# Decoder trunk in fp32 on one core: group norms by a matrix of ones, the first output projection in two halves, both first mixers reordered, a state update tied behind the weight splits

## The chip, the cores and the metric

One core of a Trainium2 chip. Time is device microseconds (us) of one execution of the whole program. TensorE does matrix products, VectorE (DVE), ScalarE (ACT) and GpSimd (POOL) elementwise work; SyncE (SP) issues the loads, POOL the stores. Each engine works through its own queue in order and waits there for what an instruction needs from others.

## What is computed

One step of a four-layer decoder: 256 prompt tokens and 8 single tokens of running sequences (264 columns together), width 1024. Layers: RWKV-7, gated linear attention (GLA), short convolution, multi-scale pooling, each followed by a squared-ReLU MLP of width 4096. The parts that the change touches:

```python
# RWKV-7: 16 heads of 64; S is a head's 64 x 64 state
def step(S, inp):
    r_t, w_t, k_t, v_t, a_t, b_t = inp
    sa = jnp.einsum('bhvk,bhk->bhv', S, a_t)
    S = S * w_t[:, :, None, :] + sa[..., None] * b_t[:, :, None, :] + v_t[..., None] * k_t[:, :, None, :]
    return S, jnp.einsum('bhvk,bhk->bhv', S, r_t)
...
mean = jnp.mean(y, axis=-1, keepdims=True)            # over a head's 64 channels
var = jnp.mean(jnp.square(y - mean), axis=-1, keepdims=True)
yn = ((y - mean) * lax.rsqrt(var + RWKV_GN_EPS)).reshape(B, L, D) * ln_w + ln_b
out = ((yn + bonus) * g) @ wo
...
h = h + out
h = h + jnp.square(jax.nn.relu(rmsnorm(h, norm_ffn[i], NORM_EPS) @ w_up)) @ w_down
```

## The kernel before

Activations lie with channels on partitions: 8 tiles of 128 channels by 264 columns, a `slab` holding four of them. All tiles called slab share one pool of 32 buffers; weights pass through `wr` (tag wraw) and `wh` (tags whi, wlo), three buffers each, nine in all. TensorE's accumulators are eight banks, three tagged `acc` and five `ps`.

Most projections use a split form (`mm3`): a weight block of 512 KB is loaded (wraw), rounded to a high part (whi, `put`, L180) and its remainder (wlo, `tt`, L188), usually on ScalarE and VectorE, and three matmuls of 264 columns add up high x high, high x low and low x high. The projections k, v and r of the first mixer (`proj_full`) instead use plain fp32 matmuls, which the trace shows as two records each.

Instructions are emitted by Python generators in the order of a plan, and a scheduler then fixes the order in each engine's queue, with the order of emission as priority among what it takes to be ready. In `RWKV_PLAN` a letter names a generator and each occurrence advances it by a step: X, V, R mix the operands of the projections k, v, r; h and G belong to the gate; s solves the triangular systems; S and O are state and output steps of a chunk of 64 tokens; D, Y, n, l serve the decode tokens; N is a group norm. `RWKV_ENGINES` and `GLA_ENGINES` say by site and number which engine takes an elementwise operation (A, V or G for ACT, DVE, POOL). `GLA_PLAN` hangs such steps behind the four parts of each pair of projections; s, o, u, l there are split, output, update and load of the decode states, A the attention blocks, L and K their decay factors (gZQ and gEX).

The group norm (`gnorm(g)`, L848 on) works on three groups of columns, group 0 (tokens 0 to 127), group 1 (128 to 191 and the decode tokens) and group 2 (192 to 255): centre by a matmul (`cen`, tile pc), square, sum each head's 64 channels into 16 rows (`sel`, tile pv), take the reciprocal root on 16 partitions (`rsq`: logarithm and exponential on ACT, three closing operations on DVE, L362 to L364), spread it over 128 partitions (`spread`, tile pr), copy, multiply, apply weight, bias and gate, and split the result into the parts xh and xl that `mixer_out` (L408) feeds to `wo_proj`. Its results go with `norm_prep` into the MLP's input X; `ffn` begins with `rstd` over the squares.

`decode_update` (L930) updates the decode tokens' state in four quarters of five DVE operations each on 128 x 1024 elements (L938 to L946). It is advanced by one step per pair of the first MLP's up projection (`next(self.later)`). It loads a quarter's state (wS) when the quarter before begins, and stores each when done.

## Time and profile before

| | us |
|---|---|
| median of three runs | 1348.36 (1346.07 to 1354.53) |
| the profiled execution | 1348.23 |
| its span, first to last instruction | 1346.5 |
| TensorE busy | 1290.8 |
| VectorE busy | 908.5 |
| ScalarE busy | 573.0 |
| GpSimd busy | 399.5 |

In the rows, PE is TensorE's matmuls and PEld its weight loads, DVE VectorE, ACT ScalarE, POOL GpSimd; L with a number is a line of the program above, and where a helper records the operation (put, tt) many operations share a line and are told apart by their tiles. Tile names stand as out<-in. "x16" counts instructions. A matmul is pipelined: its length in a row is longer than the distance to the next one. PEclk is the clock granted to TensorE as a share of full speed. Behind `<-` stands what ended a wait.

### The profile page before, as it was taken

To read this page: it belongs to the slowest core of one execution; us is meant where nothing else is said; L and a number is where in the kernel's file an instruction comes from. 1 tells how busy PE (TensorE), PEld (TensorE's weight loads), DVE (VectorE), ACT (ScalarE), POOL (GpSimd) and SP (SyncE) were. 2 spreads that over 40 slices of the span, in tenths; PEclk is the share of its full clock that TensorE was granted. 3 is DMA by queue.
4 is the path that set the end of the run, shared out by engine and by line. 5 is a ranking of instruction groups with operands and counts; after the bars stand their busy time and mean duration, and the time that the engine had idled before them with its cause. 6 is when DMAs were issued, how large, how long until landed. Compare 5 with 4: busy or idle time off the path is not lost.

```text
span 1346.5 us, 25575 instructions
## 1 busy us (share of the span) xinstructions
PE 1290.8 (96%) x10332; PEld 1237.0 (92%) x10332; DVE 908.5 (67%) x1392; ACT 573.0 (43%) x931; POOL 399.5 (30%) x420
## 2 busy tenths in 40 slices
...
GB/s 275 95 115 74 48 49 9 111 176 194 190 215 204 174 142 109 141 172 117 175 181 186 184 177 183 175 178 170 179 186 178 183 256 128 126 181 180 188 176 92
DMA packets 161880, 211.10 MB, mean 157 GB/s; under 512 B 11569, under 2 KB 116945, under 8 KB 161762
## 3 DMA queue, kind: packets, MB, share of 16 engines
...
## 4 chain that ended last, share of the span: by engine, by line
PE 80%; DVE 7%; DMA 5%; issue 3%; POOL 2%; SPq 1%; ACT 1%; DVEq 0%; ACTq 0%; POOLq 0%
PE dacc L234 11%; PE dacc L232 11%; PE dacc L233 11%; PE acc L232 10%; PE acc L234 10%; PE acc L233 10%; PE acc L272 5%; DMA wS<-in_state_wkv 2%; DVE wlo L188 1%; DMA wraw<-in_ffn_up 1%; DMA g1a<-in_rwkv_g 1%; PE pr L866 1%; PE pss L373 1%; PE pAr L802 1%; PE pQ L761 1%
## 5 line engine op out<-in xcount | busy, mean ns | idle before, releaser
L188 DVE TENSOR_TENSOR wlo<-wraw,whi 128x1024 fp32r<-128x1024 f32 x318 | 400.7, 1263 | 225.6 <-ACT whi L180 224.3
L180 ACT CAST whi<-wraw 128x1024 fp32r<-128x1024 f32 x319 | 333.6, 1049 | 407.9 <-PE dacc L233 183.1
L234 PE MATMUL acc<-xh,wlo 128*128 128x264 f32 x1408 | 398.8, 287 | 8.5 <-DVE wlo L188 8.4
L232 PE MATMUL acc<-xh,whi 128*128 128x264 f32 x1408 | 397.1, 286 | 2.9 <-DVE ggs L1145 2.7
L233 PE MATMUL acc<-xl,whi 128*128 128x264 f32 x1408 | 399.4, 286 | 0.0
L233 PE MATMUL dacc<-sl,whi 128*128 128x264 f32 x1024 | 288.9, 284 | 0.0
L232 PE MATMUL dacc<-sh,whi 128*128 128x264 f32 x1024 | 288.0, 284 | 0.0
L234 PE MATMUL dacc<-sh,wlo 128*128 128x264 f32 x1024 | 284.2, 284 | 1.4 <-DVE wlo L188 1.4
L234 PEld LDWEIGHTS acc<-xh,wlo 128*128 128x128 f32 x1408 | 264.7, 189 | 11.3 <-DVE wlo L188 10.0
L232 PEld LDWEIGHTS acc<-xh,whi 128*128 128x128 f32 x1408 | 264.0, 189 | 6.2 <-DVE ggs L1145 3.1
L233 PEld LDWEIGHTS acc<-xl,whi 128*128 128x128 f32 x1408 | 265.4, 189 | 0.6
L403 POOL TENSOR_TENSOR fs<-ft 128x264 f32<-128x264 f32 x128 | 135.6, 1063 | 262.6 <-DVE ft L399 257.5
L233 PEld LDWEIGHTS dacc<-sl,whi 128*128 128x128 f32 x1024 | 192.7, 188 | 0.0
L232 PEld LDWEIGHTS dacc<-sh,whi 128*128 128x128 f32 x1024 | 192.5, 188 | 0.0
L234 PEld LDWEIGHTS dacc<-sh,wlo 128*128 128x128 f32 x1024 | 190.0, 188 | 1.6 <-DVE wlo L188 1.6
L346 POOL TENSOR_TENSOR sq<-sq 128x264 f32<-128x264 f32 x40 | 36.8, 920 | 382.8 <-ACT sq L342 382.0
L272 PE MATMUL acc<-xm,wfull 128*128 128x264 f32 x384 | 89.1, 388 | 0.0
L272 PEld LDWEIGHTS acc<-xm,wfull 128*128 128x128 f32 x384 | 72.0, 190 | 13.7 <-issue 1.9
L399 DVE SCALAR_TENSOR_TENSOR ft<-acc,rstd 128x264 f32<-128x264 f32 x128 | 54.0, 427 | 37.5 <-PE acc L234 37.2
L404 DVE TENSOR_TENSOR sl<-fs,sh 128x264 fp32r<-128x264 f32 x128 | 58.0, 470 | 26.7 <-POOL fs L403 26.7
L401 ACT ACTIVATE sh<-ft 128x264 fp32r<-128x264 f32 x128 | 51.1, 420 | 47.2 <-DVE ft L399 44.9
L233 PE MATMUL dacc<-xl,whi 128*128 128x264 f32 x192 | 53.8, 289 | 1.0 <-POOL xl L188 0.7
...
## 6 DMA issues: line engine op xcount, KB each, us to landing
wraw<-in_ffn_up SPq DMA_DIRECT2D x128, 512.0 KB, 3.7
wraw<-in_ffn_down SPq DMA_DIRECT2D x128, 512.0 KB, 3.3
wraw<-in_gla_w_in SPq DMA_DIRECT2D x24, 512.0 KB, 3.7
wraw<-in_conv_w_in SPq DMA_DIRECT2D x24, 512.0 KB, 3.4
wfull<-in_rwkv_wk SPq DMA_DIRECT2D x8, 512.0 KB, 8.4
wfull<-in_rwkv_wv SPq DMA_DIRECT2D x8, 512.0 KB, 4.7
...
wfull<-in_rwkv_wr SPq DMA_DIRECT2D x8, 512.0 KB, 3.5
```

The costliest lines, as they stand in the source:

```text
L180: return e.copy(out, x) if scale is None else e.activation(out, x, AF.Copy, scale=scale)
L188: return self.on(site, i).tensor_tensor(out, x, y, op=op)
L232: mm(acc, h, xh, start=first, stop=False)
L233: mm(acc, h, xl, start=False, stop=False)
L234: mm(acc, l, xh, start=False, stop=last)
L272: self.nc.tensor.matmul(accs[mi][:, :NT], w[:, kk, mi * 128:(mi + 1) * 128], self.at(X, k), start=(k == 0), stop=(k == 7))
L346: self.nc.gpsimd.tensor_tensor(ss[0], ss[0], sq, op=ALU.add)
L373: nc.tensor.matmul(pp[:, :NT], self.C("ones"), x, start=f, stop=l)
L399: nc.vector.scalar_tensor_tensor(t, acc, 0.0, rs, op0=ALU.max, op1=ALU.mult)
L401: nc.scalar.activation(h, t, AF.Square)
L403: nc.gpsimd.tensor_tensor(s, t, t, op=ALU.mult)
L404: nc.vector.tensor_tensor(l, s, h.bitcast(F32), op=ALU.subtract)
```

## The change

Four things are done together. The group norm sums each head's squares with the block matrix of ones `blk`, which leaves the sum on all of its head's partitions; the reciprocal root is then taken on 128 partitions for four tiles at once, and spreading and copying fall away. The result stays fp32, unsplit. The output projection of the first mixer becomes `out_part(h)` with plain fp32 matmuls, once for columns 0 to 127 (U in the plan, eight steps among the norms of groups 2 and 1) and once for the other 136 (B, eight steps at the end); the eight weight blocks (128 columns each) are loaded in the first half and kept for the second. Each half sums its squares, makes its part of the reciprocal root `rsf` and writes its part of the MLP's input. The update of the decode state gets an order: none of its operations may be placed ahead of the low part of the last split emitted before it; two quarters are loaded at the end of the mixer, the others when a quarter has been stored. The plans and the engine strings of the first two mixers change; for the site zq, for instance, POOL's turns go from the third, fourth and eighth to the fourth and seventh, for ek from the third, fifth, seventh and eighth to the third, seventh and eighth, and xs goes from POOL, DVE to DVE, DVE.

```diff
@@ -224,7 +224,7 @@
     def wsplit(self, w, shape, place=None, site=("A", "V"), i=0):
         h, l = [place(shape, n, F32R) if place else self.wh.tile(shape, F32R, name=n, tag=n) for n in ("whi", "wlo")]
         self.put(site[0], i, h, w)
-        self.tt(site[1], i, l, w, h.bitcast(F32), ALU.subtract)
+        self.lo_ins = self.tt(site[1], i, l, w, h.bitcast(F32), ALU.subtract)
         return h, l
 
     def mm3(self, acc, h, l, xh, xl, first, last):
@@ -384,7 +384,7 @@
 
     def ffn(self, li, ss, X, next_prep, between):
         nc = self.nc
-        rs = self.rstd(ss)
+        rs = self.rstd(ss) if isinstance(ss, list) else ss
         up, down = self.I["ffn_up"][li], self.I["ffn_down"][li]
         sh = [self.slab([128, 4, NT], "sh", F32R) for _ in range(8)]
         sl = [self.slab([128, 4, NT], "sl", F32R) for _ in range(8)]
@@ -425,26 +425,26 @@
 
...
 RWKV_PLAN = """
-G R X h X X e X x0 R l0 X x1 X z z h x2 X h X z h a z z h a h a x3 x4 k0 h a k1 a a k1 k0 k1 a k1 a h z z z R t k0
-d5 d4 d2 k0 d3 R d6 d1 R k2 K0 d0 V V R k2 R V k2 R V k2 V d7 k3 V V V K0 v0 K0 v0 v0 I0 k3 k3 k3 v0 K1 v1 I0 v1 v1
-K1 I0 v1 K1 v2 v2 w00 v2 I1 v2 v3 I1 v3 v3 r0 v3 r0 I1 w01 r0 w10 y0 r0 s b1 b0 r1 r1 T100 T000 s r1 r1 w11 r2 r2 r2
-s b3 g3 r2 r3 b2 r3 s T001 r3 T101 b4 g2 s r3 b7 g4 T010 b5 g7 s l1 s D0 D1 b6 T011 g0 T110 y1 l2 g6 s S00 w21 S01
-S01 g1 S00 S01 T111 l3 O0 w30 S00 S11 w20 D2 O0 S10 D0 w31 S11 S10 S11 S21 D2 D3 D3 O1 w41 S10 w40 S21 S21 S20 S20
-S20 O2 O2 S30 D1 g5 S31 S31 O1 S30 S31 N0 S30 N0 Y P n O3 O3 N1 N1 N0 N1 N2 N2 N2 N0 N2 N1
+h X X X X X X h G R e a h X X x0 R l0 h x1 z h z h z x2 h z a z z a x3 x4 k0 a h k1 a a k1 k0 k1 a k1 a z z R t k0
+d5 d4 d2 k0 d3 V R d6 d1 R k2 K0 V d0 V R k2 R V k2 R V k2 V d7 k3 V V K0 v0 K0 v0 v0 I0 k3 k3 k3 v0 v1 K1 I0 v1 v1
+I0 K1 v1 v2 K1 v2 w00 v2 I1 v2 v3 I1 v3 w10 v3 r0 v3 I1 r0 r0 y0 r1 r1 w11 r0 s b1 b0 r1 r1 r2 T000 s r2 b2 r2 s b3
+g3 T100 r2 r3 r3 w01 s T001 r3 T101 b4 g2 s r3 b7 g4 T010 b5 g7 s l1 s D0 b6 D1 g0 T011 T110 l2 g6 s y1 S00 w21 T111
+S01 S01 w30 g1 S00 S01 S00 S11 l3 w20 S10 w31 S11 S10 D2 S11 O0 O0 S10 D0 S21 w41 D2 S21 S20 O1 w40 S21 S20 S31 S20
+S30 O1 g5 N0 D3 S30 O2 D3 N0 S31 S31 S30 N0 O3 O2 O3 D1 Y N0 N2 U n U N2 P N2 N1 U N2 N1 U U U N1 U N1 U B B B B B B
+B B
 """
 
 
@@ -834,7 +834,7 @@
         V.scalar_tensor_tensor(at(bg, m), at(bg, m), k.P("lnb", m), pg, op0=ALU.add, op1=ALU.mult)
         k.put("gT", m, at(gT, m), pg, k.P("lnw", m))
 
-    Y = k.new_x()
+    Y = two("yo")
 
 
     GROUPS = (((0, 128),), ((128, 64), (NP, NS)), ((192, 64),))
@@ -854,26 +854,20 @@
             mm(pc[a], k.C("cen"), y_tile(g, a), start=True, stop=True)
             A.activation(q[a], pc[a], AF.Square)
         yield
-        pv = k.bank("pv")[0:16, :n]
-        for m in range(8):
-            mm(pv, sel[:, m], at(q, m), start=(m == 0), stop=(m == 7))
-        r, x, c = [k.t(nm, [16, n]) for nm in ("gnr", "gnx", "gnc")]
-        k.rsq(r, pv, 1.0 / 64, k.epsg[0:16], 64e-5, c, x)
+
+        rc = [k.slab([128, 2, 4, n], "gnr") for _ in range(2)]
+        for a in range(2):
+            pv = k.bank("pv")[:, :4 * n].rearrange("p (m t) -> p m t", m=4)
+            mm(pv, k.C("blk"), q[a], start=True, stop=True)
+            k.rsq(rc[a][:, 0], pv, 1.0 / 64, k.epsg, 64e-5, rc[a][:, 1], rc[a][:, 0])
         yield
         for a in range(2):
-            pr = k.bank("pr")[:, :4 * n].rearrange("p (m t) -> p m t", m=4)
-            for mi in range(4):
-                mm(pr[:, mi], spread[:, 4 * a + mi], r, start=True, stop=True)
-            k.put("gq", g * 2 + a, q[a], pr)
-            V.tensor_tensor(q[a], pc[a], q[a], op=ALU.mult)
+            V.tensor_tensor(q[a], pc[a], rc[a][:, 0], op=ALU.mult)
             at0 = 0
             for i, (lo, w) in enumerate(GROUPS[g]):
                 xv, cs, j = q[a][:, :, at0:at0 + w], slice(lo, lo + w), g * 4 + a * 2 + i
                 k.tt("gg", j, xv, xv, gT[a][:, :, cs], ALU.mult)
-                k.tt("gb", j, xv, xv, bg[a][:, :, cs], ALU.add)
-                h, l = Y[0][a][:, :, cs], Y[1][a][:, :, cs]
-                k.put("gh", j, h, xv)
-                k.tt("gl", j, l, xv, h.bitcast(F32), ALU.subtract)
+                k.tt("gb", j, Y[a][:, :, cs], xv, bg[a][:, :, cs], ALU.add)
                 at0 += w
             yield
 
@@ -929,23 +923,28 @@
 
     def decode_update():
 
-        decode_load(0)
+
+        def op(out, x, y, o):
+            k.queue_after(V.tensor_tensor(out, x, y, op=o), k.lo_ins)
+
+        for qv in range(2):
+            decode_load(qv)
         yield
         for qv in range(4):
-            if qv < 3:
-                decode_load(qv + 1)
             S, vs, T = wS[qv], slice(qv * 16, (qv + 1) * 16), [k.slab([128, 16, 64], "wT") for _ in range(2)]
-            V.tensor_tensor(T[0], vb(vt[:, 4, vs]), kb(3), op=ALU.mult)
+            op(T[0], vb(vt[:, 4, vs]), kb(3), ALU.mult)
             yield
-            V.tensor_tensor(T[1], vb(sav[:, vs]), kb(2), op=ALU.mult)
+            op(T[1], vb(sav[:, vs]), kb(2), ALU.mult)
             yield
-            V.tensor_tensor(T[0], T[0], T[1], op=ALU.add)
+            op(T[0], T[0], T[1], ALU.add)
             yield
-            V.tensor_tensor(S, S, kb(1), op=ALU.mult)
+            op(S, S, kb(1), ALU.mult)
             yield
-            V.tensor_tensor(S, S, T[0], op=ALU.add)
+            op(S, S, T[0], ALU.add)
             for h2 in range(2):
                 k.store(Sdst[h2][:, :, qv * 1024:(qv + 1) * 1024], S[OWN[h2]].rearrange("p v k -> p (v k)"))
+            if qv < 2:
+                decode_load(qv + 2)
             yield
 
     def decode_rotate():
@@ -1038,6 +1037,36 @@
         for par in range(2):
             k.store(O["wkv_p"][OWN[par]], XV[4][par][OWN[par], :, 0, :])
 
+
+
+    wo, Xf = {}, k.new_x()
+    rsf = k.t("rsf")
+
+    def out_part(h):
+        cs, n = ((slice(0, 128), 128), (slice(128, NT), NT - 128))[h]
+        ss = []
+        for m in range(8):
+            if h == 0:
+                wo[m] = k.wfull(I["rwkv_wo"][:, m * 128:(m + 1) * 128].rearrange("(k p) c -> p k c", p=128), [128, 8, 128])
+            acc = k.bank("dacc", "ps" if m % 2 else "acc")[:, :n]
+            for kk in range(8):
+                mm(acc, wo[m][:, kk, :], at(Y, kk)[:, cs], start=(kk == 0), stop=(kk == 7))
+            x, xh, xl, g, sq = k.hT[:, m, cs], at(Xf[0], m)[:, cs], at(Xf[1], m)[:, cs], k.P("ffn0", m), k.t("sq", [128, n])
+            V.tensor_tensor(x, acc, x, op=ALU.add)
+            A.activation(sq, x, AF.Square)
+            if m in (0, 6, 7):
+                ss.append(sq)
+            else:
+                G.tensor_tensor(ss[0], ss[0], sq, op=ALU.add)
+            A.activation(xh, x, AF.Copy, scale=g)
+            V.scalar_tensor_tensor(xl, x, g, xh.bitcast(F32), op0=ALU.mult, op1=ALU.subtract)
+            if m == 7:
+                p = k.bank("pss")[:, :n]
+                for i, y in enumerate(ss):
+                    mm(p, k.C("ones"), y, start=(i == 0), stop=(i == 2))
+                k.rsq(rsf[:, cs], p, 1.0 / 1024, k.eps6, 1e-6, k.t("rsc", [128, n]), k.t("rsq", [128, n]))
+            yield
+
     def pair(n, X, pr, evac):
         if FULL[n]:
             return k.proj_full(I["rwkv_w" + n], pr * 256, X, lambda mi, acc: evac(pr * 2 + mi, acc))
@@ -1047,34 +1076,35 @@
     work = {"e": decay_low, "z": decay_logs, "a": rates, "X": lambda: operand(2, "k", Xk), "h": gate_in, "t": table, "d": decays, "K": keys, "I": inner,
             "V": lambda: operand(3, "v", Xv), "R": lambda: operand(0, "r", Xr), "s": solve, "b": after_r, "T": transposed, "G": gate_load,
             "g": gate, "w": values, "x": new_xv, "y": decode_rows, "l": decode_load, "D": decode, "Y": decode_out, "n": decode_rotate, "N": gnorm, "S": state_step,
-            "O": output_step, "P": state_out, "k": lambda i: pair("k", Xk, i, ev_k),
+            "O": output_step, "P": state_out, "U": lambda: out_part(0), "B": lambda: out_part(1), "k": lambda i: pair("k", Xk, i, ev_k),
             "v": lambda i: pair("v", Xv, i, ev_v), "r": lambda i: pair("r", Xr, i, ev_r)}
     k.issue(work, RWKV_PLAN)
     k.later = decode_update()
-    return k.mixer_out(I["rwkv_wo"], 0, Y)
+    next(k.later)
+    return rsf, Xf
 
 
 GLA_ENGINES = {
-    "gwh": "VAAAVVVAAAAVVVAAVAAAAVVV", "gwl": "VVVGGVVGGVVGGVVGGVGVVGGG", "lsh": "VV", "lsl": "VG", "zq":
-    "VVGGVVVG", "ek": "VVGVGVGG", "att": "VAAAAA", "xs": "GV", "ax": "A", "kt": "AV", "vt": "AAVVAVAA", "ot":
-    "VVVA", "sp": "AA", "sh": "AVAVAVAAAAAAAAGV", "sl": "VVVGGVVGGVVGVGGV", "km": "AGVVGVAVGAVVGVGV", "nq": "GGVG",
-    "go": "GVVGVGGG", "gy": "VVGGVVGG", "yh": "VVVVAAVA", "yl": "GGGGVGGG",
+    "gwh": "VAAAVVVAAAAVVVAAVAAVAVVV", "gwl": "VVVGGVVGGVVGGVVGGVGGVGGV", "lsh": "VA", "lsl": "VG", "zq":
+    "VVVGVVGV", "ek": "VVGVVVGG", "att": "VAAAAA", "xs": "VV", "ax": "A", "kt": "AV", "vt": "AAVVAAAA", "ot":
+    "AVVA", "sp": "VA", "sh": "AGAVAVAAVAAAAAAV", "sl": "VVVGGVVGGVVGVGGV", "km": "AGVVGVAAGAVVVVVV", "nq": "GGGV",
+    "go": "VGVGVGGG", "gy": "VVVGGVGG", "yh": "VVVVAAVA", "yl": "VGGGVGGG",
 }
 
 GLA_PLAN = [
     ("q0", "", "", "", "G"),
     ("q1", "", "Z0", "", ""),
-    ("k0", "", "", "l0", "Z1 L00 L01 K01"),
-    ("k1", "", "", "Z2", "L10"),
-    ("v0", "", "", "", "L02 L11 K11 D"),
+    ("k0", "", "", "l0", "Z1 L00 L01 K01 Z2"),
+    ("k1", "", "", "L10", ""),
+    ("v0", "", "", "", "D L02 L11 K11"),
     ("v1", "", "k", "L03", "K00"),
-    ("v2", "K02", "L12", "A17 K03 A02 l1 l2 K12 A03 A01 s01 K10 A00", ""),
-    ("v3", "", "V1 A06 l3 A04 A05 L13", "s11 s00 s21 o00 W0 F K13", "A10 s10 o01 s20 W1 u00 o11 o10 s31 l4"),
-    ("g0", "o21 X", "u10 u11 A13 s30 u01 A16 s41 A12 l5 s40 s51 l6 o20 s50 u30 o31 s60 o30 l7 o40 o41", "u20 A15 u21 u31 s61 s71", "u40 V0 A14 u50 V3 u51 o50 u41 A11"),
-    ("g1", "s70 A07 u60 V2 Y u70 o60 T1 O1 O0 o70", "", "N0 T0 N1 O2 o51 o61 o71 u61 u71 a0 a1 M0 M1", ""),
-    ("g2", "N2 O3 N3", "b M2 c M3 g3", "", "g0 g1"),
-    ("g3", "g2 g5", "", "g4 S0", ""),
-    ("wo", "g7 g6 S1"),
+    ("v2", "K02", "L12 K10 l1", "A17 K03 A02 l2 K12 A03 A01 s01", "A06 A00 V1"),
+    ("v3", "", "l3 A04 A05 L13", "s00 o00 W0 l4 F K13 s11", "s10 s31 o01 o11 s20 W1 s21 u00 o10"),
+    ("g0", "o21 A10 X", "u10 u11 A13 s30 u01 A16 s41 A15 l5 s40 s51 l6 o20 s50 u30 o31 s60 o30 l7 o40 o41", "u20 A12 u50 u21 u31 s61 s71", "u40 A14 V0 u41 A11 o50 A07"),
+    ("g1", "s70 u60 V2 Y u70 o60 O0 T1 O1 o70", "u51 N1", "N0 O2 o51 o61 o71 u61 V3 u71 a0 a1 M0", "N2 M1 b"),
+    ("g2", "O3 N3", "M2 c M3 g3", "T0", "g0 g1"),
+    ("g3", "g2 g5", "", "g4", "g6"),
+    ("wo", "S1 g7 S0"),
 ]
 
 
```

## Rows read from the trace of the kernel before

**Rows 1.** Page, part 1: engine, busy us, share of the span, instructions.

```profile
PE 1290.8 (96%) x10332; PEld 1237.0 (92%) x10332; DVE 908.5 (67%) x1392; ACT 573.0 (43%) x931; POOL 399.5 (30%) x420
```

**Rows 2.** Stretches: length, busy us of PE, PEld, DVE, ACT, POOL, clock, DMA share, GB/s.

```profile
150.00:211.00 61.00, 55.64 (x858) 48.42 (x857) 52.96 (x101) 24.07 (x61) 28.05 (x29) 0.92 0.13 36
211.00:243.00 32.00, 27.88 (x265) 22.64 (x265) 17.35 (x44) 9.04 (x24) 7.38 (x9) 0.80 0.12 30
243.00:269.50 26.50, 26.50 (x201) 26.19 (x201) 19.89 (x33) 12.27 (x22) 7.71 (x9) 0.92 0.38 118
269.50:384.00 114.50, 104.58 (x837) 102.71 (x836) 94.95 (x125) 50.63 (x73) 39.23 (x40) 1.00 0.65 189
384.00:480.00 96.00, 96.00 (x786) 95.65 (x785) 49.11 (x52) 39.89 (x51) 10.91 (x10) 1.00 0.60 194
...
510.00:565.00 55.00, 47.12 (x355) 43.46 (x354) 50.10 (x50) 17.63 (x41) 43.93 (x28) 0.94 0.38 116
565.00:592.00 27.00, 18.93 (x147) 17.43 (x146) 17.54 (x38) 7.99 (x18) 5.90 (x8) 0.81 0.54 177
```

**Rows 3.** Chain of waits, 90 to 275 us: start, length, work, records.

```profile
110.62 1.78 PE pA L706 x16
```

**Rows 4.** Chain of waits, 211 to 247 us: centring matmuls of groups 0, 1, 2.

```profile
211.03 1.06 PE pc L854 x2
...
224.63 1.17 PE pc L854 x4
...
231.67 2.00 PE pc L854 x4
```

**Rows 5.** Lines, 195 to 262 us: work, shapes, count, busy us, mean ns, idle before.

```profile
L868 DVE TENSOR_TENSOR gn<-pc,gn 128x512 f32<-128x512 f32 (+2 forms) x6 | 3.1, 523 | 0.7 <-ACT gn L180 0.6
...
L182 DVE CAST xh<-gn 128x256 fp32r<-128x256 f32 (+2 forms) x6 | 3.0, 494 | 0.9 <-POOL gn L188 0.6
...
L362 DVE SCALAR_TENSOR_TENSOR gnx<-pv,gnc 16x128 f32<-16x128 f32 (+2 forms) x3 | 0.7, 237 | 7.2 <-ACT gnc L361 7.2
```

**Rows 6.** Page, part 6: DMA issues, KB each, median us to landing.

```profile
wraw<-in_ffn_up SPq DMA_DIRECT2D x128, 512.0 KB, 3.7
...
out_gla_s<-gSs POOLq DMA_DIRECT2D x8, 512.0 KB, 4.7
...
g1a<-in_rwkv_g SPq DMA_DIRECT2D x1, 512.0 KB, 11.5
```

**Rows 7.** Lines of the weight loads (PEld), 88 to 130 us.

```profile
L706 PEld LDWEIGHTS pA<-AKa,BK 128*128 128x128 f32 x48 | 5.8, 192 | 0.2
```

**Rows 8.** Lines of DVE, 90 to 243 us.

```profile
L188 DVE TENSOR_TENSOR wlo<-wraw,whi 128x1024 fp32r<-128x1024 f32 x3 | 3.6, 1215 | 0.0
```

**Rows 9.** Waits of PE, 269.5 to 384 us: total us, times, longest us.

```profile
PE acc L234 <- DVE wlo L188: 8.4, 5, 2.8
PE dacc L234 <- DVE wlo L188: 1.4, 1, 1.4
```

**Rows 10.** Lines of DVE, 269 to 460 us.

```profile
L944 DVE TENSOR_TENSOR wS<-wS,vt 128x1024 f32<-128x1024 f32 x4 | 4.9, 1223 | 9.4 <-DMA wS<-in_state_wkv 9.4
```

**Rows 11.** Timeline of DVE, 506 to 520 us: start, length, instruction.

```profile
506.55 1.07 DVE L188 TENSOR_TENSOR gZQ<-gEX,qT 128x896 f32<-128x896 f32 x1
...
513.69 3.21 DVE L188 TENSOR_TENSOR gZQ<-gEX,qT 128x896 f32<-128x896 f32 x1
...
516.82 2.05 DVE L1320 TENSOR_TENSOR gst<-kT,gst 128x32 fp32r<-128x32 f32 x1
```

**Rows 12.** Timeline of POOL, 506 to 520 us.

```profile
515.91 2.92 POOL L188 TENSOR_TENSOR gZQ<-gEX,qT 128x896 f32<-128x896 f32 x1
```

**Rows 13.** Waits of PE, 480 to 645 us.

```profile
PE gos L1380 <- ACT gSq L180: 8.1, 2, 7.0
...
PE gks L1322 <- DVE gqkx L1317: 3.0, 1, 3.0
```

**Rows 14.** Timeline of ACT, 567 to 582 us.

```profile
578.92 0.62 ACT L180 CAST gSq<-gSs 128x512 fp32r<-128x512 f32 x1 [6.93 <-DMA out_gla_s<-gSs]
```

More of the change, by code (lines that the diff above doesn't have):

```diff
@@ L427 @@
     "u": "VV", "du": "VG", "mix0": "VAGVVAVV", "mix2": "VVVVVVVG", "mix3": "VVVVVVVV", "mix5": "VVVAGAVV", "hi0":
-    "VVVGVVGA", "lo0": "VGVGGGVV", "hi2": "AVVVVVVA", "lo2": "GGAGGGGV", "hi3": "AAVGVGGA", "lo3": "GVGVGVVV",
+    "VVGGVVGA", "lo0": "VGVGGGVV", "hi2": "AVVVVVVA", "lo2": "GGAGGGGV", "hi3": "AAVGVGGA", "lo3": "GVGVGVVV",
     "whk": "AAAVVVAA", "wlk": "VGVVGGVV", "whv": "VVVVVVVA", "wlv": "GGVAVGVG", "whr": "AVAVAAVA", "wlr":
-    "GVVGGGGG", "kk": "AAAVVAAV", "ka": "VGVAAVGG", "dcl": "GV", "vec": "GAGGGAGV", "ak": "GVVVVVGG", "ak1":
@@ L436 @@
-    "bgx": "VVVVVVVV", "am": "VVVVVVVVVVVVVVVV", "sd": "GGGVGGVGGGVGGGGG", "sa": "AVAVAAAAAAAAAAAV", "ys":
-    "VVVVAVAAVAAVAAAA",
+    "GVVGGGGG", "kk": "AAAVVAAA", "ka": "VGVAAVGG", "dcl": "AV", "vec": "GAGGGAGV", "ak": "GVVVVVGG", "ak1":
+    "GAGVAVGG", "bb": "VGGGVVVV", "bk": "VVVVVGVG", "xd": "VVAVAVAAAAAAAAAV", "xt": "VAVAAAAAAAAVAAVA", "mt":
+    "AAVAGAAV", "mq": "VAAAVVVA", "v": "AAVVAVAA", "vec4": "AVVVAVGV", "rb": "AGAGGVVAAAAAAGVA", "vec5": "AVVAAAAV",
+    "bd": "AAAVAGAVAVGGAAAAAAVGAAVAAAAGAAAA", "bt": "AAAAAAVA", "gT": "AVAAAAAV", "gg": "VGVGVVVGVGVV", "gb":
```

8 lines of the change are left out of this document (3 added, 5 removed).

## The prediction

> **What bounds the kernel.** I read the page first, then the stretches (busy time and granted clock), then the waits of TensorE stage by stage, then the chain and the single instructions where it waited. TensorE is busy 96% of the span [rows 1], so only time in which it stands idle, or runs on the lower of its two clock levels (1.2 instead of 2.4 GHz), can be won; work that is moved or sped up on another engine is worth what it takes out of such a place. In a healthy stretch, the second half of the first MLP, 786 recorded matmuls fill 96.0 us, 122 ns each, without a gap [rows 2]. I call lost: idle, plus the busy time multiplied by what is missing of the granted clock. By that measure four places of the stretches lose time [rows 2]. The solve and the state steps (150 to 211): 5.4 idle and 0.08 x 55.6 = 4.4, together 9.8 us. The end of the first mixer (211 to 269.5): 4.1 idle, 0.20 x 27.9 = 5.6, and 0.08 x 26.5 = 2.1, together 11.8 us. The up projection of the first MLP (269.5 to 384): 9.9 us idle at full clock. The second mixer (510 to 592): 7.9 + 8.1 idle and 2.8 + 3.6 of clock, 22.4 us. The sum is made against the profiled execution, 1348.23 us with a span of 1346.5 (1.7 us lie around it); the median of the runs is 1348.36, so a difference taken from this trace can be read off the median.
>
> **First mixer's end, the norms.** A group norm loses its 16-row sums and the spreading back. Both streamed 128, 72 and 64 columns, 16 records (two to a matmul) for each size: 2 x 16 x 264 columns. A record of 128 columns with a new weight each time takes 1.78 / 16 = 0.111 us [rows 3], 0.87 ns a column, so 7.3 us go. The matrix of ones streams the same shapes as the centring matmul: twice 1.06, then 1.17, then 2.00 at half clock, so 1.0 [rows 4]: 4.3 us come. Net -3.0 us of TensorE.
>
> VectorE: the three closing operations of each rsqrt grow from 16 partitions to 128 x 512, 288 and 256. That is the shape of the product at L868, 3.1 us for its six [rows 5], so 9.3 us come; the three small ones (0.7 each, 2.1 together) and the rounding xh (3.0) go [rows 5], and with them the low parts and the copies of the spread result. I count the two as equal. ScalarE gets the wider logarithm and exponential; it was busy 9.0 of 32 us here [rows 2], which hides their sum; the chain of each norm becomes somewhat longer.
>
> **First mixer's end, the projection.** Out go 192 matmuls of 264 columns in the split form, 192 x 0.122 = 23.4 us. In come 64 plain fp32 matmuls on 128 columns (128 records x 0.111 = 14.2) and 64 on 136 columns (128 x 0.111 x 136/128 = 15.1): 29.3 us, so +5.9. TensorE's work in this stretch at full clock was 58.5 - 11.8 = 46.7 and becomes 46.7 + 5.9 - 3.0 = 49.6 us. The point of the halves is that the first one needs only group 0, and can run while the chains of groups 1 and 2 go through ScalarE and VectorE; there the engine now waits and falls to the half clock (pc of 256 columns needs 2.00 us where the longer 288 needed 1.17 [rows 4]). I leave 1.5 us lost, near the lower bound of nothing, since 14.2 us of ready work stands against 4.1 us of idle: 58.5 - 51.1 = **7.4 us won**. Bounds: nothing lost, 8.9 won; all idle and all half clock stay, 5.9 - 3.0 = 2.9 lost.
>
> Costed at nothing: the weights of the projection, eight loads as before but in rows of 128 columns, can be asked for as soon as the last dense projection frees its buffers, before the state steps begin; what this shape can cost when the queues are full is the 11.5 us of g1a, also 128 columns wide [rows 6], which that lead of over 60 us hides. The eight blocks then hold eight of the nine weight buffers until the second half has used them. The MLP's first loads queue on SP behind that release, and all its later loads behind them. Its first block can be asked for after the first of eight steps, 13 us before the MLP starts, and lands in 3.7 [rows 6]; with the cover gone the start would wait about those 3.7 us and the split. The elementwise work of the residual is done in 16 pieces of half size instead of 8, under 15 us of matmuls.
>
> The same form with changing weights comes every 111 ns although its load is shown as 192 ns long [rows 3, 7], so on this trace loads run beside the matmuls. A rule speaks against the plain form at 128 columns: the Trainium skill, page "TensorE: Matmul & The Clock Gate", section "Back-to-back issue gap", says that in a stream of weight load and matmul both set the spacing, and its section "LDWEIGHTS" gives 107 ns for 128 columns. By it, if loads came on top, the sum would be an estimated 256 x 107 ns = 27 us higher; the trace does not agree.
>
> **First mixer's middle.** The split of the projection's weights goes. Three of the eight low parts ran on VectorE between 90 and 243 us, 3.6 us together [rows 8], in the stretch where VectorE works on the solve that the state steps wait for (52.96 of 61 us busy [rows 2]). A gain between nothing and 3.6 us; I take **2**, the middle, because TensorE still has other work at that time. The new order of the plan before the solve I cost at nothing: there TensorE is bound by the dense projections. If the gate projection, now first, went to the head of its queue, the k projection would stand behind the late g1a, at most its 11.5 us.
>
> **First MLP.** TensorE waits only for wlo: 8.4 + 1.4 = 9.8 us [rows 9]. VectorE in turn stood 9.4 us in front of the decay of the state (L944), on the load of wS [rows 10]: it is the in-order queue that puts the split behind a DMA. The change asks for two quarters before the MLP (four issues on SP, ahead of the MLP's weights, in the last steps of the mixer) and for the next two when a quarter is stored, some fifteen operations ahead, and ties each update to a place after the last split made. The five operations per quarter stay. At the least nothing is gained, if the loads still come late; at most 9.9. Since each operation takes 1.2 us [rows 10] and may still stand before a split, I take **8 us**.
>
> **Second mixer.** Here the plan is shuffled and operations change engines. On this trace a VectorE operation next to one of POOL is stretched: the gZQ that takes 1.07 us alone takes 3.21, and a 32-column gst takes 2.05, both beside POOL's own gZQ of 2.92 [rows 11, 12]; TensorE then waits 3.0 us for gqkx [rows 13]. The change takes this gZQ (the third of the string zq), one gEX and one gXS off POOL. That is worth about the 3.0 us less one gZQ of 1.07, 2 us, and the other two as much again: 4 us. The longest wait, 7.0 us for gSq [rows 13], is ScalarE waiting for a store of gSs to finish before it may write a buffer [rows 14]; the order moves loads and splits around, and I see nothing that gives this wait a reason to go or to come. So **4 us**, with ends 15 won (both gos and gks waits and the clock lost with them) and 14 lost (two more store waits).
>
> Sum: 7.4 + 2 + 8 + 4 = 21.4; 1348.2 - 21.4 = **1327 us**.
>
> **Rivals.** (a) The half projection does not fill: the 9.3 us of wide closing operations are late in VectorE's queue, the first half starts when the chains are over, TensorE still drops to the half clock. For it: 9.3 us of new closing operations stand in the one queue that also serves the state steps; against it: VectorE is busy 37.2 of these 58.5 us. 1327 + 7.4 + 2.9 = 1337; chance 0.13. (b) The reordered second mixer runs free: 1327 - 11 = 1316; 0.13. (c) One or two more store waits in the second mixer, since loads and splits move earlier while the buffers are the same: 1327 + 4 + 7 to 14 = 1338 to 1345; 0.12. (d) The first MLP keeps its waits, because the later two loads queue on SP behind weights that wait for buffers: 1335; 0.07. (e) Weight loads set the pace of the plain projection: 256 x (192 - 111) ns = 20.7, 1348; against it [rows 3]; 0.03. The page named above is what speaks for it. (f) Slower: the store waits of (c) become the rule, as there are eight stores of gSs [rows 6] whose buffers are wanted again. From three more waits of 7.0 us on (4 + 21 against 21.4) the change loses; with four, 1327 + 4 + 28 = 1359. For it: the wait is there already; against it: nothing makes the stores slower or more; 0.04. The forecast keeps 0.48, with its own range of 1320 to 1334.
>
> **Numbers.** A measurement of this kernel can tell about 1% from no change, 13.5 us, so faster is under 1335. Nearly all of the forecast, (b), and the edges of (a) and (d) lie there: 0.68. Slower by over 1% needs (f) with five waits or more: 0.03. The rest, 0.29, is the same. The range 1312 to 1341 leaves out the far part of (b), half of (c), (e) and (f): 0.2.
>
> **What would show it.** Right: the first half's matmuls lie between the group norms, granted clock above 0.95 from the norms to the MLP, the MLP's first matmul 9 us earlier; no wait of L944 on wS; the wait for gqkx near 1 us. Wrong: TensorE idle between the last state step and the first half; a wait of gos on gSq of 7 us more than once; spacing over 120 ns inside the halves.

## The result and the profile after

The changed kernel takes 1316.6 us (1313.0 to 1317.6 in four runs) against 1347.8 for the kernel before, measured beside it: a ratio of 0.975, interval 0.972 to 0.979. That is 10.4 us below the predicted 1327, inside the range of 1312 to 1341 and outside the forecast's own range of 1320 to 1334; it is where rival (b), the second mixer running free, had put it. Its profiled execution took 1313.0 us with a span of 1311.2, so the two profiles show 35.2 us of gain where the medians show 31.2.

Page, part 1 (engine, busy us, share, instructions), beside [rows 1]:

```profile
PE 1276.8 (97%) x10318; PEld 1224.9 (93%) x10318; DVE 897.5 (68%) x1398; ACT 571.4 (44%) x949; POOL 381.3 (29%) x415
```

Stretches of the kernel after; the columns are those of [rows 2]. The end of the first mixer is 200 to 256.4, its MLP's up projection 256.4 to 367, the second mixer's inner part 492 to 574 (510 to 592 before).

```profile
150.00:200.00 50.00, 46.14 (x713) 40.36 (x715) 42.13 (x86) 21.47 (x54) 19.36 (x22) 0.90 0.12 34
200.00:222.00 22.00, 20.00 (x305) 15.33 (x301) 20.69 (x31) 9.47 (x22) 11.73 (x11) 1.00 0.07 13
222.00:256.40 34.40, 34.12 (x280) 32.76 (x281) 22.65 (x63) 14.62 (x41) 7.51 (x14) 1.00 0.32 97
256.40:367.00 110.60, 105.74 (x846) 103.69 (x845) 95.66 (x128) 50.10 (x75) 37.85 (x40) 1.00 0.66 191
...
492.00:547.00 55.00, 48.52 (x385) 45.56 (x385) 51.63 (x59) 19.14 (x44) 40.35 (x28) 0.97 0.41 136
547.00:574.00 27.00, 26.30 (x214) 24.01 (x214) 23.40 (x48) 10.93 (x25) 13.36 (x14) 1.00 0.60 207
```

The end of the mixer, where [rows 2] had a granted clock of 0.80 and 0.92, runs at full clock with 0.3 us idle in its last 34 us. The up projection idles 4.9 us instead of 9.9. The largest change is at the bottom: by the prediction's measure (idle, plus busy time multiplied by what is missing of the clock) the second mixer's inner part lost 22.4 us before and loses 6.5 + 1.5 + 0.7 = 8.7 now.

All kernels of this study can be laid side by side by three marks of TensorE's records: when the first MLP's up projection starts, how long that MLP lasts (to the last matmul of its down projection), and how long it is from there to the first matmul of the second MLP's down projection (the second mixer and an up projection that loses nothing). Each row is one profiled execution; the median beside it is of all runs. Single executions scatter: after, g_old, g_eng, g_plan and g_zq have the same first mixer and start the first MLP between 256.4 and 261.0 us (granted clock from 222 to 240 us 1.00 in the first, 0.91 in the last), so a few us in the second column mean little by themselves.

| kernel | first MLP starts | first MLP lasts | second mixer and up | median us | ratio to before |
|---|---|---|---|---|---|
| before | 269.5 | 200.6 | 279.0 | 1347.8 | 1 |
| after | 256.4 | 195.5 | 261.8 | 1316.6 | 0.972 to 0.979 |
| g_old | 259.9 | 194.4 | 275.5 | 1328.6 | 0.982 to 0.988 |
| g_eng | 257.9 | 194.3 | 267.1 | 1315.0 | 0.973 to 0.978 |
| g_plan | 258.3 | 196.3 | 266.9 | 1319.8 | 0.976 to 0.980 |
| g_zq | 261.0 | 193.4 | 261.3 | 1314.6 | 0.972 to 0.979 |
| b_gla | 272.2 | 203.8 | 261.5 | 1336.2 | 0.987 to 0.992 |
| u_last | 257.2 | 192.8 | 261.3 | 1313.9 | 0.970 to 0.975 |
| u_full | 268.8 | 195.0 | 261.8 | 1325.8 | 0.980 to 0.987 |
| plan_old | 261.8 | 198.8 | 260.9 | 1316.6 | 0.970 to 0.978 |
| b_blk | 267.8 | 201.2 | 279.1 | 1346.9 | 0.995 to 0.999 |
| upd_free | 267.2 | 199.5 | 262.4 | 1327.4 | 0.981 to 0.988 |
| load_all | 258.4 | 193.2 | 262.4 | 1313.3 | 0.970 to 0.975 |
| best | 262.8 | 193.9 | 261.2 | 1310.7 | 0.970 to 0.977 |

From before to after the profiles differ by 13.1 at the first mark (1.0 of it already at the first dense matmul, 22.5 to 21.5 us), 5.1 in the first MLP, 17.2 in the second mixer, and -0.1 in all the rest: 35.3 us of span. The prediction had 9.4, 8 and 4.

### The profile page after: what moved, and what is told of

Read it like the earlier page. It is cut to its first block, busy times and chain, and to the rows that moved or that the text cites. A ratio compares the mean times of both kernels' runs of the same rounds, so it can differ in the third digit from the quotient of the medians.

```text
span 1311.2 us, 25583 instructions
## 1 busy us (share of the span) xinstructions
PE 1276.8 (97%) x10318; PEld 1224.9 (93%) x10318; DVE 897.5 (68%) x1398; ACT 571.4 (44%) x949; POOL 381.3 (29%) x415
## 4 chain that ended last, share of the span: by engine, by line
PE 83%; DVE 10%; DMA 2%; issue 2%; ACT 1%; POOL 0%; DVEq 0%; SPq 0%; ACTq 0%; POOLq 0%
PE acc L232 11%; PE acc L234 11%; PE acc L233 11%; PE dacc L234 11%; PE dacc L233 11%; PE dacc L232 11%; PE acc L272 5%; DMA wraw<-in_ffn_up 2%; PE dacc L1053 2%; DVE wlo L188 1%; PE pss L373 1%; DVE zt L736 1%; DVE Zs L738 1%; PE pQ L761 1%; PE gE L1215 0%
## 5 line engine op out<-in xcount | busy, mean ns | idle before, releaser
L188 DVE TENSOR_TENSOR wlo<-wraw,whi 128x1024 fp32r<-128x1024 f32 x310 | 390.8, 1263 | 227.8 <-ACT whi L180 226.9
L180 ACT CAST whi<-wraw 128x1024 fp32r<-128x1024 f32 x310 | 324.4, 1049 | 405.0 <-PE dacc L233 176.8
L233 PEld LDWEIGHTS dacc<-sl,whi 128*128 128x128 f32 x1024 | 192.8, 188 | 0.0
L346 POOL TENSOR_TENSOR sq<-sq 128x264 f32<-128x264 f32 x35 | 32.6, 932 | 361.1 <-ACT sq L342 360.6
L399 DVE SCALAR_TENSOR_TENSOR ft<-acc,rstd 128x264 f32<-128x264 f32 x96 | 40.9, 428 | 38.8 <-PE acc L234 38.6
L342 ACT ACTIVATE sq<-hT 128x264 f32<-128x264 f32 x56 | 23.5, 419 | 37.8 <-DVE hT L383 35.5
```

Of the source, the lines that this page charges most:

```text
L180: return e.copy(out, x) if scale is None else e.activation(out, x, AF.Copy, scale=scale)
L188: return self.on(site, i).tensor_tensor(out, x, y, op=op)
L233: mm(acc, h, xl, start=False, stop=False)
L346: self.nc.gpsimd.tensor_tensor(ss[0], ss[0], sq, op=ALU.add)
L399: nc.vector.scalar_tensor_tensor(t, acc, 0.0, rs, op0=ALU.max, op1=ALU.mult)
```

## Experiments on the second mixer

The miss lies here, so four kernels take its order and its engine string apart. g_old puts both back as in the minus lines of the change's diff, g_eng only `GLA_PLAN`, g_plan only `GLA_ENGINES`; b_gla is the kernel before with nothing but the two new ones. In short:

```diff
 GLA_ENGINES = {
...
-    "VVVGVVGV", "ek": "VVGVVVGG", "att": "VAAAAA", "xs": "VV", "ax": "A", "kt": "AV", "vt": "AAVVAAAA", "ot":
+    "VVGGVVVG", "ek": "VVGVGVGG", "att": "VAAAAA", "xs": "GV", "ax": "A", "kt": "AV", "vt": "AAVVAVAA", "ot":
...
 GLA_PLAN = [
...
-    ("v2", "K02", "L12 K10 l1", "A17 K03 A02 l2 K12 A03 A01 s01", "A06 A00 V1"),
+    ("v2", "K02", "L12", "A17 K03 A02 l1 l2 K12 A03 A01 s01 K10 A00", ""),
```

g_old:

> The changed kernel with the second mixer's order and engine string of the kernel before; all else as changed. From the start of the second mixer to the first matmul of its MLP's down projection the kernel before took 279.0 us, the changed one 261.8. If those 17.2 us come from the second mixer's own edits, this kernel takes 1316.6 + 17 = 1334 us and its stretch is 279 us again. If they came from what stands ahead (the state update's stores and loads gone earlier, so that the second mixer's own loads find a free queue), it stays near 1317 and the stretch near 262.

g_eng:

> The changed kernel with the second mixer's order of before but the new engine string. If the gain of the second mixer is what the operations taken off GpSimd give (the forecast's 4 us: less stretching beside each other, a shorter wait for gqkx), the time is that of the old string less 4, about 1330, and the 7 us wait of gos on gSq stays. If the gain were mostly of the engines, 1318 to 1322. If of the order alone, 1333 to 1335.

g_plan:

> The changed kernel with the second mixer's new order but the engine string of before. If the order carries the gain (state loads and splits earlier, so that a buffer's store has ended before the next load wants it, and dense work between the steps), 1317 to 1321, with no 7 us wait of gos on gSq. If the engines carry it, 1330 or more, with VectorE operations of 3.2 us beside GpSimd ones again. If the two only work together, both this kernel and the one with the engines alone lie above 1326.

b_gla:

> The kernel before with nothing changed but the second mixer's order and engine string. If the second mixer's gain stands by itself, 1348 - 17 = 1331 us. If it needs the changed first mixer and first MLP (an earlier end of the state update's stores), 1340 or more. By the forecast's term for this part, 1344.

Measured, in this order: 1328.6, 1315.0, 1319.8 and 1336.2. Only g_plan lies in one of its expected cases; g_eng is faster than all of its own, g_old and b_gla lie between theirs. The second mixer's own edits are worth 12 us in the changed kernel and 13.6 in the kernel before, so the gain stands by itself. It doesn't add up from two halves: the new string alone on the old order brings 13.6, the new order alone on the old string 8.8, both together 12. With the order alone TensorE meets a new wait, for an evacuation that the old string keeps on VectorE (waits of TensorE in g_plan, 450 to 620 us: total, times, longest):

```profile
PE acc L232 <- DVE vT L1164: 7.6, 1, 7.6
```

Is it the three operations that the prediction named? g_zq is g_old with the sites zq, ek and xs alone as changed (`vt` and all else as before). GpSimd has three operations less by it, one gZQ, one gEX and one gXS, and the last of its remaining gZQ moves from the eighth turn to the seventh:

```diff
-    "VVGGVVVG", "ek": "VVGVGVGG", "att": "VAAAAA", "xs": "GV", "ax": "A", "kt": "AV", "vt": "AAVVAVAA", "ot":
+    "VVVGVVGV", "ek": "VVGVVVGG", "att": "VAAAAA", "xs": "VV", "ax": "A", "kt": "AV", "vt": "AAVVAVAA", "ot":
```

> The changed kernel with the second mixer's order of before and its engine string of before, save the three sites named in the forecast: one gZQ, one gEX and one gXS taken off GpSimd. The old order took 1328.6 us with the old string and 1315.0 with the new one, so the string is worth 13.6. If the three operations off GpSimd are that, 1315 to 1318. By the forecast's 4 us, 1324 to 1325. If it is the rest of the string (evacuations moved between VectorE and ScalarE, the later GpSimd sites), 1327 to 1329.

Measured: 1314.6, against 1328.6 for g_old. These turns alone, in the old order, carry as much as the whole new string (13.6) or string and order together (12). The two kernels reach the second mixer at the same time (454.3 and 454.4 us), so their traces can be read side by side. Stretches of g_old and of g_zq:

```profile
500.00:570.00 70.00, 56.23 (x426) 52.13 (x424) 58.68 (x75) 21.34 (x45) 43.72 (x33) 0.93 0.43 138
570.00:640.00 70.00, 65.91 (x499) 63.22 (x499) 59.25 (x103) 36.14 (x70) 38.73 (x36) 0.98 0.42 145
```

```profile
500.00:570.00 70.00, 64.60 (x526) 60.61 (x525) 65.18 (x99) 24.42 (x52) 50.02 (x36) 0.98 0.49 166
570.00:626.00 56.00, 53.69 (x408) 51.50 (x406) 48.69 (x82) 33.96 (x62) 31.46 (x31) 1.00 0.45 149
```

Lost in g_old: 13.8 + 3.9 + 4.1 + 1.3 = 23.1; in g_zq: 5.4 + 1.3 + 2.3 = 9.0. The difference, 14.1, is the difference of the two stretches, 275.5 less 261.3, about 10 of idle and 4 of clock. Where it comes from stands in GpSimd's queue (timeline of POOL: start, length, instruction), of g_old and of g_zq:

```profile
510.62 2.27 POOL L188 TENSOR_TENSOR gXS<-gXS,kT 128x512 f32<-128x512 f32 x1
512.85 1.15 POOL L1329 TENSOR_TENSOR gpick<-gpick,cst 24x8 f32<-24x8 f32 x1
...
529.76 2.31 POOL L188 TENSOR_TENSOR gZQ<-gEX,qT 128x896 f32<-128x896 f32 x1
...
555.72 0.68 POOL L213 DMA_DIRECT2D out_gla_s<-gSs  x1 [6.91 <-DVE gSs L1396]
```

```profile
504.00 1.14 POOL L1329 TENSOR_TENSOR gpick<-gpick,cst 24x8 f32<-24x8 f32 x1
...
547.84 0.67 POOL L213 DMA_DIRECT2D out_gla_s<-gSs  x1 [1.51 <-DVE gSs L1396]
```

In g_old the small gpick stands behind the large gZQ and gXS and runs 8.9 us later. VectorE's gkm reads it (timeline of DVE, g_old and g_zq):

```profile
514.03 6.69 DVE L184 TENSOR_SCALAR gkm<-gks,gpick 128x256 fp32r<-128x256 f32 x8
```

```profile
511.05 2.71 DVE L184 TENSOR_SCALAR gkm<-gks,gpick 128x256 fp32r<-128x256 f32 x6
...
514.03 0.34 DVE L184 TENSOR_SCALAR gkm<-gks,gpick 128x256 fp32r<-128x256 f32 x1
```

The chain of g_old goes gXS, gpick, eight gkm, attention masks, TensorE; and once more through GpSimd's operations behind the gZQ at 529.8 (gEX, wlo, gsv, gvs, gSq, from 535.0 us on). The first updated state can be stored 7.9 us later than in g_zq, and the buffers of the states, which the later steps want, come free as much later. That is what the long wait on a store was (timeline of ACT in g_old, beside [rows 14]):

```profile
561.22 0.62 ACT L180 CAST gSq<-gSs 128x512 fp32r<-128x512 f32 x1 [4.89 <-DMA out_gla_s<-gSs]
```

In g_zq no ScalarE instruction of this kind waits for a store. g_plan bears this reading out from the other side: the three operations are still GpSimd's there, but the new order puts gpick ahead of the gZQ and the gXS that it stands behind in g_old, and the first store goes 6.7 us earlier than in g_old (timeline of POOL in g_plan; its second mixer starts at 454.6 us, g_old's at 454.3):

```profile
503.98 0.20 POOL L1329 TENSOR_TENSOR gpick<-gpick,cst 24x8 f32<-24x8 f32 x1
...
507.27 2.06 POOL L188 TENSOR_TENSOR gZQ<-gEX,qT 128x896 f32<-128x896 f32 x1
509.30 1.25 POOL L188 TENSOR_TENSOR gXS<-gXS,kT 128x512 f32<-128x512 f32 x1
...
549.05 0.68 POOL L213 DMA_DIRECT2D out_gla_s<-gSs  x1 [4.53 <-DVE gSs L1396]
```

No gSq of ScalarE waits for a store there either, and 8.8 us are gone. All 14 profiles fall in the same two groups: gpick 57 to 59 us and the first store 101 to 104 us after the mixer's start in before, g_old and b_blk (275.5 to 279.1 us in the table), gpick at 49 to 50 and the store at 91 to 98 in the others (260.9 to 267.1). What is shown is that these turns of GpSimd are enough for the gain, and that the new order alone gets most of it without them; that both work through what is queued behind the large operations is read from these rows. Which of the three operations does most, and what the move of the last gZQ adds, is open.

## Experiments on the first mixer's end

u_last moves the eight U of the plan behind the last N; u_full takes the projection in one piece; plan_old keeps the new code with the old order and engine string of the first mixer; b_blk is the kernel before with only the new group norm.

u_last:

```diff
...
-S30 O1 g5 N0 D3 S30 O2 D3 N0 S31 S31 S30 N0 O3 O2 O3 D1 Y N0 N2 U n U N2 P N2 N1 U N2 N1 U U U N1 U N1 U B B B B B B
...
+S31 S20 S30 O1 g5 N0 D3 S30 O2 D3 N0 S31 S31 S30 N0 O3 O2 O3 D1 Y N0 N2 n N2 P N2 N1 N2 N1 N1 N1 U U U U U U U U B
...
```

> The changed kernel, its first mixer's plan with all eight steps of the first half projection moved behind the last norm, ahead of the second half; nothing interleaved. The forecast holds that the ready matmuls of the first half fill the chains of norms 2 and 1, where the kernel before lost 9.7 us (4.1 idle, 5.6 at half clock). If so, the mixer ends 6 to 9 us later than in the changed kernel, with half clock among the norms again: 1323 to 1326 us. If the gain of the tail is that of the shorter norms alone, and the scheduler fills anyway, the same time within 2 us.

plan_old (the old `RWKV_PLAN`, with the new letters behind it; the lines of the engine string are left out):

```diff
...
-S30 O1 g5 N0 D3 S30 O2 D3 N0 S31 S31 S30 N0 O3 O2 O3 D1 Y N0 N2 U n U N2 P N2 N1 U N2 N1 U U U N1 U N1 U B B B B B B
...
+S20 S20 O2 O2 S30 D1 g5 S31 S31 O1 S30 S31 N0 S30 N0 Y P n O3 O3 N1 N1 N0 N1 N2 N2 N2 N0 N2 N1 U U U U U U U U B B
...
```

> The changed kernel with the first mixer's plan and engine string of before (the same letters in the old order, both halves of the projection appended). If the new order and engines of the first mixer, which the forecast costed at nothing but 2 us for the middle, carry some of its 13 us, this kernel ends its mixer by that much later than the one with only the first half moved to the end: by the forecast 0 to 2 us, so 1324 to 1328; were the order worth 3 or more, 1329 or more.

b_blk:

```diff
-        pv = k.bank("pv")[0:16, :n]
...
+        rc = [k.slab([128, 2, 4, n], "gnr") for _ in range(2)]
...
+            mm(pv, k.C("blk"), q[a], start=True, stop=True)
+            k.rsq(rc[a][:, 0], pv, 1.0 / 64, k.epsg, 64e-5, rc[a][:, 1], rc[a][:, 0])
```

> The kernel before with only the group norm changed to the matrix of ones (result still split, projection as before). By the forecast TensorE sheds 3.0 us of matmuls and the closing operations on 128 partitions come in the place of small ones: VectorE +9.3, -2.1 here (the rounding stays). If TensorE's work decides, 1345; if the chain of each norm decides (pv to the product), the logarithm and exponential on 128 x 512 instead of 16 rows and three wide closing operations make it longer, 1350 or more; if the four spread matmuls and the copy that fall away shorten it, 1342.

u_full (and the letters N to the end without B):

```diff
-        cs, n = ((slice(0, 128), 128), (slice(128, NT), NT - 128))[h]
+        cs, n = slice(0, NT), NT
...
-            if h == 0:
+            if True:
```

> The changed kernel with the output projection of the first mixer in one piece: the same plain fp32 matmuls, 64 of 264 columns (128 records) in the place of 64 of 128 and 64 of 136, behind the last norm. Moving the first half's letters to the end of the plan had changed nothing, because the scheduler still placed its matmuls between the norms; here nothing of the projection is ready there. If the halves' filling is what won the tail, TensorE stands idle or at half clock among the norms again and the first MLP starts 6 to 9 us later than in the changed kernel, near 264 to 267 us: total 1322 to 1325. If the tail's gain is that of dropping the split, its operations and the spread, the MLP starts within 2 us of the changed kernel's 256 to 258, total 1315 to 1318.

u_last took 1313.9 us. It didn't test what it was to test: in TensorE's queue 32 of the first half's 64 matmuls (64 records, from 223.0 us on) still stand ahead of the last norm's sums at 233.0, since the scheduler places what is ready. So the letters' place in the plan is worth nothing. u_full, where nothing is ready, does test it, and took 1325.8, 9.2 us more than the changed kernel. Its stretches, and TensorE's waits from 200 to 270 us:

```profile
222.00:238.00 16.00, 6.95 (x21) 4.09 (x20) 13.58 (x34) 5.45 (x13) 2.21 (x4) 0.70 0.14 42
238.00:268.80 30.80, 30.73 (x129) 26.00 (x130) 10.72 (x18) 7.70 (x17) 6.10 (x8) 0.93 0.41 120
```

```profile
PE dacc L1052 <- POOL yo L188: 5.0, 1, 5.0
PE pys L954 <- DVE vt L921: 4.1, 1, 4.1
```

TensorE is busy 7 of 16 us among the norms, at a clock of 0.70. The halves fill exactly this. b_blk took 1346.9, 0.1 to 0.5% less than before: the norm's form alone is worth 0.9 to 6.5 us. plan_old came out level with the changed kernel by the median (four runs from 1312.9 to 1320.3), not at the 1324 to 1328 expected, while its profile starts the first MLP 5.4 us later. One trace of the order is seen: from the first to the last matmul of the dense projections k, v and r it is 124.6 to 126.4 us in the ten kernels with the new order and engines and 126.6 to 128.4 in the four with the old ones, plan_old among them, 2.0 us by the means. Whether it reaches the total is left open.

## Experiments on the first MLP

upd_free lets the update's operations float again, with the loads as changed; load_all asks for all four quarters in the mixer; best joins load_all with u_last.

upd_free:

```diff
-            k.queue_after(V.tensor_tensor(out, x, y, op=o), k.lo_ins)
+            V.tensor_tensor(out, x, y, op=o)
```

> The changed kernel without the tie: the update's operations may again be placed by the scheduler ahead of the low part of the last split; the loads two quarters ahead as changed. The stretch of the first MLP took 200.6, 201.2 and 203.8 us in the three kernels with the old update and 192.8 to 196.3 in those with the new one. If the loads alone took VectorE out of its wait, as the forecast says, 193 to 196 us and the same total, 1314 to 1318. If the tie carries it, because an operation of 1.2 us placed ahead of a split delays TensorE, 198 us or more and 1319 to 1323. No 9 us wait of the state's decay on wS in either case.

Measured: 1327.4, 10.8 us more, above both expected ranges, and the wait on wS, expected in neither case, is there. With the loads early, the tie carries the gain, and in two places. In the first MLP, 199.5 us long, the old waits return (waits of VectorE, then of TensorE, 255 to 480 us):

```profile
DVE wS L928 <- DMA wS<-in_state_wkv: 9.8, 2, 4.9
```

```profile
PE acc L234 <- DVE wlo L188: 6.0, 3, 2.8
```

The larger cost is ahead of it. One of the update's operations was placed between the last norm's product and its result yo, which the first half waits for, and a second soon behind it (timeline of DVE):

```profile
244.60 0.44 DVE L865 TENSOR_TENSOR gn<-pc,gnr 128x288 f32<-128x288 f32 x1
247.46 1.22 DVE L928 TENSOR_TENSOR wS<-wS,vt 128x1024 f32<-128x1024 f32 x1 [2.41 <-DMA wS<-in_state_wkv]
248.60 0.42 DVE L188 TENSOR_TENSOR yo<-gn,bg 128x256 f32<-128x256 f32 x1
...
250.07 1.63 DVE L928 TENSOR_TENSOR wS<-wS,vt 128x1024 f32<-128x1024 f32 x1 [0.26 <-DMA wS<-in_state_wkv]
```

VectorE stands 2.4 us in front of a load that has not landed, works 1.2 on the state, and only then finishes yo. TensorE waits 3.8 us there and then runs at a clock of 0.51 from 249 to 255.5 us; the first MLP starts at 267.2, 10.8 us later than in the changed kernel. 6.7 of these come here; 4.1 are there at 228.6 us already, ahead of any of the update's operations, and are no cost of theirs. The loads two quarters ahead are the same as in the changed kernel: they don't help where the queue's order is wrong. The tie without the earlier loads was not run.

load_all (best has the same, and the plan of u_last):

```diff
-        for qv in range(2):
+        for qv in range(4):
             decode_load(qv)
...
-            if qv < 2:
-                decode_load(qv + 2)
```

> The changed kernel with all four quarters of the decode state asked for at the end of the mixer. In the changed kernel SP issues the two late loads from 316 to 319 us, and ScalarE then waits 2.9 and 5.9 us for weights at 323 and 330. If those weights are late because of the state loads in their queue, the first MLP becomes 2 to 4 us shorter: 1313 to 1315 us. If they are late for buffers of their own, no change; if four loads ahead of the MLP's first weights (512 KB each) push these back, 1319 or more.

best:

> The two variants that came out at 1313.3 and 1313.9 us in one: all four quarters of the decode state asked for at the end of the mixer, and the first half's letters behind the last norm. If both differences from the changed kernel's 1316.6 are real, 1310 to 1311; if they are within what the runs scatter, 1313 to 1316.

Measured: 1313.3 and 1310.7 (1308.2 to 1318.3 in six runs). Their ratios overlap with the changed kernel's, so neither is shown to beat it. The profile of best, an execution of 1317 us, shows what four loads ahead of the MLP's first weights may cost. SP's queue, and ScalarE's:

```profile
237.35 5.24 SPq L150 DMA_DIRECT2D wS<-in_state_wkv  x8
248.69 23.35 SPq L221 DMA_DIRECT2D wraw<-in_ffn_up  x6
```

```profile
261.71 1.04 ACT L180 CAST whi<-wraw 128x1024 fp32r<-128x1024 f32 x1 [10.21 <-issue]
```

The weights asked for at 248.7 are rounded 13.0 us later, at 261.7; in load_all it is 10.1, in the changed kernel, with two quarters ahead of them, 3.9. TensorE then waits 3.0 us for this whi and 5.1 for the squares that stand behind it in ScalarE's queue (0.8 and 1.7 in load_all, 1.2 and 0.3 in the changed kernel). That the loads are what whi waits for is read from the order on SP; the profile names no releaser. The MLP's start at 262.8 is no measure of it, since g_zq, with two quarters, starts it at 261.0; what the MLP takes (193.9 us) is no less than in other kernels with the new update.

## Why the prediction came out as it did

**The first mixer's end: 7.4 and 2 predicted.** From the last dense matmul (149.8 us before, 146.8 after) to the first MLP it took 119.7 us and takes 109.6: 10.1 against 9.4. Over before and b_gla on one side, and the five kernels with the changed first mixer as it stands on the other, the means differ by 9.5 (119.8 and 121.9; 109.6 to 112.9). The reason given holds; the middle's 2 was not run apart from the end's 7.4. Undoing the halves costs 9.2 us; the prediction's two cases, 7.4 won and 2.9 lost with all idle kept, lie 10.3 apart. The 3.0 us off TensorE by the norm's form lie in b_blk's 0.9 to 6.5. The closing operations (lines of DVE, 195 to 262 us, beside [rows 5]) take 9.2 us, for 9.3 in the sum:

```profile
L364 DVE SCALAR_TENSOR_TENSOR gnr<-gnr 128x512 f32<-128x512 f32 (+2 forms) x6 | 3.2, 543 | 0.0
L362 DVE SCALAR_TENSOR_TENSOR gnr<-pv,gnr 128x512 f32<-128x512 f32 (+2 forms) x6 | 3.0, 518 | 0.9 <-ACT gnr L361 0.9
...
L363 DVE SCALAR_TENSOR_TENSOR gnr<-gnr 128x512 f32<-128x512 f32 (+2 forms) x6 | 3.0, 516 | 0.0
```

The spacing inside the halves is what [rows 3] gave (chain of waits, 205 to 262 us):

```profile
224.91 1.78 PE dacc L1053 x16
...
235.26 5.37 PE dacc L1053 x48
...
244.85 4.42 PE dacc L1053 x38
249.28 5.04 DMA wraw<-in_ffn_up
```

That is 111 and 112 ns for 128 columns and 116 for 136, with a new weight each time; in u_full 264 columns take 240 ns (30.69 us for 128 records, at a clock of 0.93). The spacing follows the columns, no load comes on top of it, and rival (e) falls. The Trainium skill, page "TensorE: Matmul & The Clock Gate", section "Back-to-back issue gap", has loading and multiplying both set the spacing, but pipelined; loads on top, as the prediction weighed the rule, is more than the section says, and these records don't show it. The MLP's first weights were asked for 10.1 us before its start, not 13; the second block, the last row, took 5.0 us, not 3.7, and lies on the chain, but TensorE idled only 0.3 us in these 34. Two us were costed at nothing: the dense projections end 3.0 us earlier, 1.0 of it from the start; the other 2.0 are what the kernels with the new order differ by from those with the old one.

**The first MLP: 8 predicted.** The two profiles differ by 5.1, but over the table the MLP lasts 200.6, 201.2 and 203.8 with the old update, and 192.8 to 196.3 in the nine kernels with the new one behind the new first mixer (all but upd_free and plan_old); the means are 201.9 and 194.3. So 7.6, and the size was right. plan_old, with the new update behind the old order, takes 198.8; no VectorE operation waits on wS there, but TensorE waits 2.7 us for the squares at the start, and the clock up to 372 us is 0.98. With it the difference is 7.1. What failed is the reason: the prediction named the tie, but hung the gain on the loads (nothing gained "if the loads still come late") and counted the operations' place only as what is left over ("may still stand before a split"). With the loads early and no tie, in upd_free, the wait on wS is back at 9.8 us and the MLP at 199.5: the loads alone don't remove it. What is left of TensorE's wait in the changed kernel (255 to 480 us, beside [rows 9]):

```profile
PE acc L234 <- DVE wlo L188: 1.8, 4, 0.7
PE acc L232 <- DVE ft L399: 1.6, 1, 1.6
PE acc L232 <- ACT whi L180: 1.2, 1, 1.2
```

**The second mixer: 4 predicted, 17 in the profiles, 12 to 14 by the medians.** This is the step that missed: the term was mis-sized, and with it the whole sum. The operations were the right ones, but each was priced by the first wait it touches ([rows 13]'s gqkx, 3.0 us). That wait is no measure: in g_zq it still stands with 3.1 us, and 14 us are gone. The stretching behind this price was partly misread, too: VectorE's gZQ of 3.21 us [rows 11] runs from 513.69 to 516.90, and up to 515.95 GpSimd was not at its gZQ [rows 12] but at a weight split (timeline of POOL before):

```profile
513.56 2.39 POOL L188 TENSOR_TENSOR wlo<-wraw,whi 128x1024 fp32r<-128x1024 f32 x1 [0.68 <-issue]
```

And the wait of 7.0 us on a store [rows 14] was put aside with "I see nothing that gives this wait a reason to go"; the reason was in the order of GpSimd's queue, which was read only for [rows 12]. Had the prediction followed the first state's store back from its issue (571.4 us before, 101 us after the mixer's start, against 92 now), it would have passed these operations. The places of the sum also ended at 592 us, while 5 us were idle from 592 to 640, 1.6 in the same stretch now. TensorE's waits there in the kernel after (450 to 640 us):

```profile
PE gks L1356 <- DVE gst L1350: 2.4, 1, 2.4
PE gA L1248 <- DVE att L1254: 1.5, 1, 1.5
PE gA L1248 <- ACT att L180: 1.5, 1, 1.5
```

**The rivals.** (a) and (d) didn't come: the halves fill, the MLP's waits are gone. (b) came, for a reason that the prediction half had; the stated range held because it was drawn to take in (b), not because the sum was right. (c) and (f), more store waits, went the other way: one wait of 3.4 us on ScalarE is left, and TensorE's longest wait for gSq is 0.6. Of the signs announced, the first half between the norms, the clock (1.00 from 200 us to the MLP), the earlier first matmul (13 us for 9) and the missing wait on wS came; the wait for gqkx near 1 us did not, its neighbour gst took its place with 2.4.
